# Emission order inside the turns of queries and keys: all high parts ahead of the differences that read them

## The chip, the cores and the metric

The kernel runs on one core of one Trainium2 chip. The core has five engines with queues of their own: TensorE (PE; its weight loads are listed as PEld), VectorE (DVE), ScalarE (ACT), GpSimd (POOL) and SyncE (SP, which issues DMAs). An engine carries out its instructions in the order of its queue; between engines, semaphores keep the order. The metric is the time of one execution on the device in microseconds, lower is better.

## The reference

Two trunk layers of a diffusion backbone with 512 latent tokens and 256 context tokens (768 rows of width 1024). Layer 0 mixes tokens by differential attention, layer 1 by neighbourhood attention with a position bias; each is followed by a dense MLP with squared ReLU.

```python
for i in range(DEPTH):                       # DEPTH = 2
    h_l = modulate(rms_norm(x, norm1_g[i]), mod_l[0], mod_l[1])
    h_c = modulate(rms_norm(ctx, norm1_g[i]), mod_c[0], mod_c[1])
    if kind == 0:
        y_l, y_c = diff_attention_mixer(h_l, h_c, p, i, cos, sin, need_ctx)
    elif kind == 1:
        y_l, y_c = neighbourhood_mixer(h_l, h_c, p, need_ctx)
...
    x = x + mod_l[2] * y_l
    x = x + mod_l[5] * squared_relu_mlp(modulate(rms_norm(x, norm2_g[i]), mod_l[3], mod_l[4]),
                                        w_mlp1[i], w_mlp2[i])
```

In differential attention each of 8 heads has two query and key maps of 64 channels (m = 0 and 1); the weights are the difference of two softmaxes. All arithmetic is float32.

```python
def diff_attend(q, k, v, lam):
    s = jnp.einsum('bqhmd,bkhmd->bhmqk', q, k).astype(jnp.float32) * ATTN_SCALE
    p = jax.nn.softmax(s, axis=-1)
    w = (p[:, :, 0] - lam * p[:, :, 1]).astype(v.dtype)
    return jnp.einsum('bhqk,bkhe->bqhe', w, v)
```

## The kernel before, in words

Float32 operands are multiplied as two parts: a high part, rounded by a copy on ACT to the type that PE takes (fp32r), and a low part, the difference of the value and its high part, made on DVE or POOL. Products of the parts are added in PSUM.

The time line has four phases. Layer 0's attention runs to about 470 us, layer 0's MLP to about 1110, layer 1's attention to about 1490, layer 1's MLP to the end. The attention phases are cut into steps of one head (layer 0, `head0`) or one pair of heads (layer 1, `group1`), for row tiles of 128 tokens:

- `Q`, project: PE multiplies a row tile with the head's weights (L408), ACT takes the sum out of PSUM (L415), squares (L419), DVE reduces (L421), POOL takes the power (L296), DVE scales (L423). Values are split on ACT and DVE (L468 and L469 in layer 0, L620 and L621 in layer 1). Layer 0 then rotates the channels, mostly on POOL (L473 to L483).
- `U`, turn: PE transposes queries and keys of two row tiles into one PSUM tile (L499 into PC; L634 and L636 into PA). `q_split` and `k_split` take them out in high and low parts. `U0`, `U2` and `U4` are the three turns of a head. In layer 0 tile PC has one buffer, so the next turn's transposes write over the last one's.
- `S`, scores: PE multiplies queries with keys (L517, L656), DVE takes the row maximum (L522, L662), ACT the exponential (L523, L663).
- `T`, `V`, `O`: the weights are transposed (L541, L686) and split (L543 and L544, L687 and L688), multiplied with the values (L552, L701), scaled or put together (L555 to L561, L708 and L709), and given out (L569, L570).
- `w` and `c`: loading and splitting the next head's weights (L129, then L145 on ACT and L146 on POOL, or on DVE in layer 1).

`q_split` and `k_split` work on two halves of 64 partitions, `lo` and `hi`, one for each map m. For queries, the high part of a half stays in its half and the difference goes into the other one. For keys, the high part is copied into both halves (L444, L446) and the difference too: the first on DVE (L445), the second on POOL as a copy of it (L450) in the turns U0 and U2, on DVE again in U4 (L448, `soon`). In layer 1 turn U0 has no queries, and the queries' parts are scaled by a gain (L436, L437). In each turn all these instructions but L450 read one PSUM tile.

The order of PE, SP and POOL is fixed by hand: strings such as `CYCLE0`, `START0` and `END0` list the steps ("U4' Q0b c1 w3 Q1a T0'"; a mark stands for an earlier head), and `run` emits them in this order. ACT and DVE are not fixed: a planner that simulates the program orders them when it is built, by when their inputs are ready and by the order of emission. It also sets all semaphores. Two engines' instructions that touch the same tile get an order from the order in which they are emitted.

Of the kernel before, what the change touches and what calls it, by code (L numbers as in the profile page):

```python
# [12 lines left out]
AF = mybir.ActivationFunctionType  # L13
# [50 lines left out]
class Block:  # L64
# [362 lines left out]
    def q_split(self, ps, q, cols, gain=None):  # L427

        nc = self.nc
        lo, hi = slice(0, 64), slice(64, 128)  # L430
        for m, (a, b) in enumerate(((lo, hi), (hi, lo))):
            if gain is None:
                nc.scalar.activation(q[a, m, cols], ps[a], AF.Copy)
                nc.vector.tensor_sub(q[b, m, cols], ps[a], q[a, m, cols].bitcast(F32))
            else:
                nc.scalar.activation(q[a, m, cols], ps[a], AF.Copy, scale=gain[a])  # L436
                nc.vector.scalar_tensor_tensor(q[b, m, cols], ps[a], gain[a], q[a, m, cols].bitcast(F32),  # L437
                                               op0=ALU.mult, op1=ALU.subtract)

    def k_split(self, ps, kh, kl, cols, soon):  # L440
        nc = self.nc
        lo, hi = slice(0, 64), slice(64, 128)
        for m, (a, b) in enumerate(((lo, hi), (hi, lo))):
            nc.scalar.activation(kh[a, m, cols], ps[a], AF.Copy)  # L444
            nc.vector.tensor_sub(kl[a, m, cols], ps[a], kh[a, m, cols].bitcast(F32))  # L445
            nc.scalar.activation(kh[b, m, cols], ps[a], AF.Copy)  # L446
            if soon:
                nc.vector.tensor_sub(kl[b, m, cols], ps[a], kh[a, m, cols].bitcast(F32))  # L448
            else:
                nc.gpsimd.tensor_copy(kl[b, m, cols], kl[a, m, cols].bitcast(F32))  # L450
# [679 lines left out]
```

## Time and profile before

| what | us |
|---|---|
| median of 3 runs | 1902.31 |
| lowest and highest run | 1901.79, 1906.84 |
| the profiled execution's own time | 1902.15 |
| its span, first to last instruction | 1899.6 |
| PE busy in the span | 1786.5 |
| DVE, ACT, POOL busy | 1133.4, 833.7, 812.6 |

An instruction's row in the profile names its line, the engine, the operation and the tiles it writes and reads ("Q<-PC": writes a tile Q, reads PC). A wait names the instruction that released the engine. "PE PS L517 <- ACT Q L446" means that PE stood still ahead of L517, which writes PS, until ACT's L446, which writes Q, was done. A stretch's row gives its length and then each engine's busy time in it.

### The profile page before, as it was taken

The page shows a single profiled execution, that of the slowest core. Times are in us where ns is not written, and L with a number is a line of the kernel's source. Part 1 is how long each engine was busy: PE and PEld are TensorE (multiplying, and loading weights), DVE is VectorE, ACT ScalarE, POOL GpSimd, SP SyncE. Part 2 cuts the span into 40 slices and gives each one's busy share as a digit, 9 for nine tenths or more (in the row PEclk, how much of TensorE's full clock was granted, in tenths as well). Part 3 has the DMA queues.
Part 4 walks back from the last instruction along what each step waited for, and adds up shares of the span by engine and source line. Part 5 has one row for each costly group of instructions (what it writes and reads, how often), then busy time and mean ns, then how long its engine had stood idle before and what let it go on. Part 6 is the DMA issues. An engine that isn't in the chain of part 4 may idle for free.

```text
span 1899.6 us, 27132 instructions
## 1 busy us (share of the span) xinstructions
PE 1786.5 (94%) x10256; PEld 1563.8 (82%) x10256; DVE 1133.4 (60%) x2158; ACT 833.7 (44%) x1854; POOL 812.6 (43%) x688
## 2 busy tenths in 40 slices
PE   6989999996999999999999998999998989999998
PEld 5878888884789888888888977989897778888886
DVE  4588777885574343343334676777777664444446
ACT  4476767774342212221221245777676342323321
POOL 3755566653224333342432432433345444444443
PEclk9999999997999999999999998999999999999999
DMA  8122222224324443443432132122212323223232
GB/s 329 42 84 78 87 87 87 79 71 169 119 73 136 132 160 111 167 162 116 148 134 85 56 100 64 57 71 74 65 67 89 117 92 97 89 91 109 90 101 76
DMA packets 66499, 197.61 MB, mean 104 GB/s; under 512 B 8192, under 2 KB 23488, under 8 KB 60224
## 3 DMA queue, kind: packets, MB, share of 16 engines
q1 hardware_dynamic: 58608, 186.03, 29.4%
q10 hardware_dynamic: 7760, 9.85, 1.5%
q8 instruction: 80, 1.31, 0.3%
q14 instruction: 51, 0.42, 0.1%
HBM read 180.74 MB, written 15.11 MB: 103 GB/s over the span
## 4 chain that ended last, share of the span: by engine, by line
PE 75%; DVE 11%; ACT 6%; issue 4%; POOL 2%; DMA 2%; ACTq 0%; SPq 0%; POOLq 0%; DVEq 0%
PE PD L830 22%; PE PA L408 14%; PE PA L865 11%; PE PB L865 9%; PE PA L750 4%; PE PA L257 2%; PE PS L517 2%; PE PB L552 2%; PE PQ L398 1%; PE PS L656 1%; PE PB L701 1%; PE PB L541 1%; PE PB L686 1%; DVE Y L423 1%; ACT W L145 1%
## 5 line engine op out<-in xcount | busy, mean ns | idle before, releaser
L146 POOL TENSOR_TENSOR W<-R,W 128x1024 fp32r<-128x1024 f32 x142 | 351.3, 2485 | 540.6 <-ACT W L145 537.0
L830 PE MATMUL PD<-Q,W 128*128 128x384 f32 (+2 forms) x1992 | 396.0, 346 | 2.4 <-DVE Q L334 1.1
L830 PEld LDWEIGHTS PD<-Q,W 128*128 128x128 f32 x1992 | 345.7, 188 | 33.7 <-issue 8.6
L145 ACT ACTIVATE W<-R 128x1024 fp32r<-128x1024 f32 (+1 forms) x172 | 172.7, 1021 | 450.7 <-PE PA L865 193.6
L865 PE MATMUL PA<-W,H 128*128 128x512 f32 x1080 | 275.4, 393 | 4.6 <-POOL W L146 3.0
L865 PEld LDWEIGHTS PA<-W,H 128*128 128x128 f32 x1080 | 200.1, 188 | 51.3 <-issue 4.5
L839 DVE TENSOR_TENSOR N<-N 128x768 f32<-128x768 f32 (+1 forms) x64 | 66.9, 1046 | 279.2 <-ACT N L835 170.4
L865 PE MATMUL PB<-W,H 128*128 128x512 f32 x840 | 209.2, 391 | 0.0
L865 PEld LDWEIGHTS PB<-W,H 128*128 128x128 f32 x840 | 157.4, 188 | 33.4
L408 PE MATMUL PA<-W,Q 128*128 128x384 f32 (+1 forms) x1008 | 174.3, 325 | 0.4 <-DVE H L621 0.4
L408 PEld LDWEIGHTS PA<-W,Q 128*128 128x128 f32 x1008 | 158.6, 191 | 0.7 <-DVE H L621 0.7
L296 POOL TENSOR_TENSOR SQ<-SQ,half 128x4 f32<-128x4 f32 (+1 forms) x96 | 94.7, 988 | 128.9 <-DVE SQ L421 127.7
L842 DVE SCALAR_TENSOR_TENSOR H<-N,H 128x768 fp32r<-128x768 f32 (+1 forms) x64 | 97.9, 1532 | 25.7 <-ACT H L841 25.0
L408 PE MATMUL PA<-WB,H 128*128 128x384 f32 x576 | 110.9, 345 | 0.8 <-DVE Q L469 0.8
L750 PE MATMUL PA<-W,H 128*128 128x512 f32 x384 | 97.5, 404 | 7.9 <-ACT H L743 5.1
L408 PEld LDWEIGHTS PA<-WB,H 128*128 128x128 f32 x576 | 101.1, 192 | 1.8 <-DVE Q L469 1.1
L830 PE MATMUL PD<-H,W 128*128 128x512 f32 (+1 forms) x408 | 94.1, 378 | 2.4 <-DVE SA L290 2.0
L876 DVE TENSOR_TENSOR H<-PA,H 128x512 f32<-128x512 f32 x78 | 53.8, 690 | 69.7 <-PE PA L865 69.7
L750 PEld LDWEIGHTS PA<-W,H 128*128 128x128 f32 x384 | 71.9, 192 | 25.9 <-ACT H L743 5.4
L523 ACT ACTIVATE E<-PS,SA 128x768 f32<-128x768 f32 (+1 forms) x96 | 72.9, 760 | 36.5 <-DVE SA L522 33.6
L830 PEld LDWEIGHTS PD<-H,W 128*128 128x128 f32 x408 | 73.8, 188 | 18.0 <-DVE H L334 2.9
L517 PE MATMUL PS<-Q,Q 128*128 128x256 f32 (+1 forms) x320 | 70.2, 352 | 19.1 <-ACT Q L446 9.9
(210 smaller groups left out, 3052.6 us busy)
## 6 DMA issues: line engine op xcount, KB each, us to landing
R<-in_w_dram SPq DMA_DIRECT2D x128, 512.0 KB
M<-in_wmod_dram SPq DMA_DIRECT2D x48, 1024.0 KB
R<-in_wqa_dram SPq DMA_DIRECT2D x32, 384.0 KB
R<-in_wqb_dram SPq DMA_DIRECT2D x32, 384.0 KB
Y<-in_rpb_dram SPq DMA_DIRECT2D x48, 128.0 KB
bias<-Y SPq DMA_DIRECT2D x48, 128.0 KB
X<-bias SPq DMA_DIRECT2D x8, 768.0 KB
R<-in_woa_dram SPq DMA_DIRECT2D x8, 512.0 KB
```

What stands on the lines that cost most here:

```text
L145: high = nc.scalar.activation(w[:, 0, :n], raw, AF.Copy)
L146: low = (eng or nc.gpsimd).tensor_sub(w[:, 1, :n], raw, w[:, 0, :n].bitcast(F32))
L296: nc.gpsimd.tensor_tensor(r, ss, self.half[:, :n], op=ALU.pow)
L408: nc.tensor.matmul(acc[:, :n], hT[kt][:, x, P * i:P * i + P], w[kt // 2][:, y, o:o + n], start=(kt == 0 and p == 0), stop=(kt == KT - 1 an ...
L517: nc.tensor.matmul(s[:, c0:c1], q[:, m, P * i:P * i + P], k[:, m, c0:c1], start=p == 0, stop=p == 1)
L523: nc.scalar.activation(e[:, m, :nk], s, AF.Exp, bias=mx[:, 0:1], accum_out=sm[:, m:m + 1])
L750: nc.tensor.matmul(ps, oHL[h][:, x, c:c + P], w[h // 2][:, y, 512 * (h % 2):512 * (h % 2) + 512], start=(first and h == hs[0] and p == 0), ...
L830: nc.tensor.matmul(ps[:, at:at + b1 - b0], w[kt // 4][:, x, o:o + P], hT[kt][:, y, b0:b1], start=(kt == 0 and p == 0), stop=(kt == KT - 1 ...
L839: nc.vector.tensor_mul(r, r, r)
L842: nc.vector.scalar_tensor_tensor(u[:, 1, :], r, 1.0, u[:, 0, :].bitcast(F32), op0=ALU.mult, op1=ALU.subtract)
L865: nc.tensor.matmul(ps, hd[:, x, P * i - c0:P * i - c0 + P], w[f][:, y, 512 * n:512 * n + 512], start=(f == 0 and p == 0), stop=(f == len(h ...
L876: nc.vector.tensor_add(av, ps, av)
```

## The change

In both helpers the copies of a turn are emitted ahead of the differences. In `q_split` the two copies come first, then the two differences. In `k_split` all four copies come first, then the differences (and POOL's copies) of the two halves. No instruction is added or removed, and none has other operands.

```diff
         lo, hi = slice(0, 64), slice(64, 128)
+        for m, a in enumerate((lo, hi)):
+            scale = {} if gain is None else dict(scale=gain[a])
+            nc.scalar.activation(q[a, m, cols], ps[a], AF.Copy, **scale)
         for m, (a, b) in enumerate(((lo, hi), (hi, lo))):
             if gain is None:
-                nc.scalar.activation(q[a, m, cols], ps[a], AF.Copy)
                 nc.vector.tensor_sub(q[b, m, cols], ps[a], q[a, m, cols].bitcast(F32))
             else:
-                nc.scalar.activation(q[a, m, cols], ps[a], AF.Copy, scale=gain[a])
                 nc.vector.scalar_tensor_tensor(q[b, m, cols], ps[a], gain[a], q[a, m, cols].bitcast(F32),
                                                op0=ALU.mult, op1=ALU.subtract)
...
         for m, (a, b) in enumerate(((lo, hi), (hi, lo))):
-            nc.scalar.activation(kh[a, m, cols], ps[a], AF.Copy)
+            for c in (a, b):
+                nc.scalar.activation(kh[c, m, cols], ps[a], AF.Copy)
+        for m, (a, b) in enumerate(((lo, hi), (hi, lo))):
             nc.vector.tensor_sub(kl[a, m, cols], ps[a], kh[a, m, cols].bitcast(F32))
-            nc.scalar.activation(kh[b, m, cols], ps[a], AF.Copy)
             if soon:
                 nc.vector.tensor_sub(kl[b, m, cols], ps[a], kh[a, m, cols].bitcast(F32))
             else:
```

## The prediction

> **What bounds the kernel now.** I read the page first, then the stretches, then the waits of TensorE (PE), then who holds up whom around the changed lines.
>
> ```profile
> PE 1786.5 (94%) x10256; PEld 1563.8 (82%) x10256; DVE 1133.4 (60%) x2158; ACT 833.7 (44%) x1854; POOL 812.6 (43%) x688
> ...
> 72.00:200.00 128.00, 114.24 (x713) 100.43 (x713) 101.14 (x237) 84.64 (x244) 77.89 (x94) 0.96 0.20 70
> 206.00:402.00 196.00, 189.97 (x1301) 175.63 (x1301) 156.64 (x375) 139.25 (x400) 115.77 (x150) 1.00 0.25 84
> 402.00:470.00 68.00, 51.32 (x298) 40.45 (x297) 47.53 (x98) 38.02 (x104) 29.08 (x34) 0.83 0.37 123
> ...
> 1206.00:1442.00 236.00, 218.30 (x1554) 212.95 (x1553) 182.61 (x420) 171.94 (x423) 97.14 (x113) 1.00 0.22 73
> ```
>
> PE is busy 94% of the span, and its order is written out by hand, so a faster turn of queries and keys pays only where PE stands still. The rows below the page line are stretches: length, then busy time of PE, PEld, DVE, ACT, POOL, then the granted clock. The first heads of layer 0 (72 to 200 us) leave PE idle for 13.8 us (128.00 less 114.24), its steady heads (206 to 402) for 6.0, its end (402 to 470) for 16.7, the steady groups of layer 1 (1206 to 1442) for 17.7. DVE works 77 to 80% of these stretches (end: 70%), so a wait in its queue reaches others.
>
> What ends PE's idle time, in four stretches: 72 to 205, 205 to 402, 402 to 470, then layer 1.
>
> ```profile
> PE PC L499 <- ACT Q L446: 3.3, 1, 3.3
> PE PS L517 <- ACT Q L446: 2.1, 2, 1.4
> ...
> PE PS L517 <- ACT Q L446: 3.7, 4, 1.1
> PE PS L517 <- DVE Q L448: 0.2, 1, 0.2
> ...
> PE PS L517 <- ACT Q L446: 4.1, 2, 2.5
> ...
> PE PB L686 <- DVE T L709: 6.7, 6, 1.4
> ...
> PE PS L656 <- ACT H L446: 1.1, 1, 1.1
> PE PS L656 <- DVE H L448: 0.3, 1, 0.3
> ```
>
> Columns: total, times, longest. L446 is the second high copy of the keys, the last piece of a turn. In layer 0 PE waits for it 3.3 + 2.1 + 3.7 + 4.1 = 13.2 us; in layer 1 hardly (1.1), there it waits for L709, an output step behind the turns in DVE's queue.
>
> Now ACT and DVE, layer 0 (72 to 440 us), same columns:
>
> ```profile
> ACT Q L446 <- DVE Q L445: 11.3, 10, 2.7
> ACT Q L444 <- DVE Q L434: 6.1, 7, 1.4
> ACT Q L433 <- DVE Q L434: 5.8, 10, 1.2
> ACT Q L444 <- DVE Q L448: 4.1, 6, 0.7
> ```
>
> A copy (L433, L444, L446) needs nothing that a difference makes: it reads PSUM tile PC and writes its own place. Yet it waits for the difference before it, 27.3 us in all. What they share is PC: its readers on two engines are kept one after another in the order in which they are emitted. One steady turn, step U4 of a head, shows the price:
>
> ```profile
> 234.56 0.60 PE L499 MATMUL PC<-ident,Y 128*128 128x128 f32 x4
> 235.20 0.38 ACT L433 ACTIVATE Q<-PC 64x256 fp32r<-64x256 f32 x1
> 235.61 0.42 DVE L434 TENSOR_TENSOR Q<-PC,Q 64x256 fp32r<-64x256 f32 x1
> 236.82 0.38 ACT L433 ACTIVATE Q<-PC 64x256 fp32r<-64x256 f32 x1
> 237.13 1.93 DVE L561 SCALAR_TENSOR_TENSOR O<-O,SO,one 128x128 f32<-128x128 f32 x1 [0.66 <-POOL SO L296]
> 239.09 0.43 DVE L434 TENSOR_TENSOR Q<-PC,Q 64x256 fp32r<-64x256 f32 x1
> 239.56 0.38 ACT L444 ACTIVATE Q<-PC 64x256 fp32r<-64x256 f32 x1 [0.68 <-DVE Q L434]
> 241.64 0.38 ACT L444 ACTIVATE Q<-PC 64x256 fp32r<-64x256 f32 x1 [0.74 <-DVE Q L448]
> 241.75 1.17 PE L517 MATMUL PS<-Q,Q 128*128 128x512 f32 x6
> 243.61 0.38 ACT L446 ACTIVATE Q<-PC 64x256 fp32r<-64x256 f32 x1
> 244.03 0.42 DVE L448 TENSOR_TENSOR Q<-PC,Q 64x256 fp32r<-64x256 f32 x1 [1.10 <-ACT Q L446]
> 244.05 0.96 PE L517 MATMUL PS<-Q,Q 128*128 128x512 f32 x2 [1.13 <-ACT Q L446]
> ```
>
> Six copies and six differences are 6 x 0.38 + 6 x 0.42 = 4.8 us of work; from the first copy to the end of the last difference it takes 235.20 to 244.45, 9.25 us. Each change of engine joins a queue that meanwhile does other work (the second L434 stands behind L561). PE reaches this head's scores at 241.75 and loses 1.13 us.
>
> **The change part by part.** No instruction is added, dropped or made longer; no DMA moves; the orders of PE, POOL and SP stay. What changes is the order in which the readers of a turn follow each other, and with it the plan for ACT and DVE. Call copies A, differences D.
>
> Steps U4: A D A D, then A D A D A D A D, 11 changes of engine; after, A A D D, A A A A D D D D, 3. U0 and U2 in layer 0: 8 become 3. The twelve-step chain alone stays at 4.8 us. What goes is queueing: 9.25 - 4.8 = 4.4 us over 11 changes, 0.4 each; with 3 changes the turn takes some 4.8 + 3 x 0.4 = 6.0 us, ending near 241.2, before PE's 241.75.
>
> Waits added: the first difference waits for the second copy as well, and the keys' first difference for all four copies. Without queueing the keys' first low half is ready at 4 x 0.38 + 2 x 0.42 = 2.4 us instead of 2 x 0.38 + 2 x 0.42 = 1.6: 0.8 later, the last one equal. Behind a held difference stand DVE's softmax steps and output steps. The trace shows no such block; below, a hold costs nothing where DVE has other work ahead of it, above, 0.8 us for each turn. I count 0 for the hold itself: PE's rows name copies, not first differences.
>
> Gains, by stretch:
> - Steady heads: 3.7 + 0.2 = **3.9 us**, all gone by the turn above. Late next is the exponential before the following scores, which PE waits for anyway.
> - First heads: the 2.1 goes likewise. The 3.3 is PE waiting to write the next turn over PC:
>
> ```profile
> 79.27 0.41 DVE L445 TENSOR_TENSOR Q<-PC,Q 64x256 fp32r<-64x256 f32 x1
> 81.69 0.38 ACT L446 ACTIVATE Q<-PC 64x256 fp32r<-64x256 f32 x1 [1.22 <-DVE Q L445]
> 82.13 1.11 PE L499 MATMUL PC<-ident,Y 128*128 128x128 f32 x4 [3.34 <-ACT Q L446]
> ```
>
>   With the copies done, both key differences run back to back from 79.27, ending about 80.1 instead of 82.07: 2.0. Together **4.1 us**.
> - End of layer 0: 4.1 us at stake. The copies come early, but differences still queue behind output steps; I take **2.5**, between 0 and 4.1.
> - Layer 1, steady. One group:
>
> ```profile
> 1248.36 0.39 ACT L415 ACTIVATE Y<-PA 128x256 f32<-128x256 f32 x1 [1.19 <-PE PA L408]
> 1248.94 0.38 ACT L446 ACTIVATE H<-PA 64x256 fp32r<-64x256 f32 x1
> 1249.32 0.38 ACT L444 ACTIVATE H<-PA 64x256 fp32r<-64x256 f32 x1
> 1249.73 0.85 ACT L145 ACTIVATE W<-R 128x768 fp32r<-128x768 f32 x1
> ...
> 1250.61 0.96 DVE L146 TENSOR_TENSOR W<-R,W 128x768 fp32r<-128x768 f32 x1 [0.45 <-ACT W L145]
> 1251.93 0.43 DVE L709 TENSOR_TENSOR T<-PB,T 64x256 f32<-64x256 f32 x1
> 1252.41 0.66 PE L686 MATMUL PB<-ident,E 128*128 128x128 f32 x4 [1.06 <-DVE T L709]
> ```
>
>   Two copies held back by differences stand ahead of L145, L146, L709 and so PE. Emitted together they fit into ACT's idle 1.19 us before L415, and the chain moves up by 1249.73 - 1248.94 = 0.79. I take 0.75 for each of the 6 waits: **4.5 us** (0 to 6.7).
> - End of layer 1: 1.1 + 0.3 = **1.4**.
>
> Sum 16.4. Against it: four copies in a row (1.52 us) where at most two stood (0.76), so ACT work behind can wait 0.76 longer in each of 48 turns, 36.5 us in all. The share that reaches PE I take as PE's largest idle share of a working stretch, 13.8 / 128 = 11%: **4.0 us**. Bounds: 0 (ACT's idle time takes it) and 36.5. Net 12.4. The profiled execution took 1902.15 us (span 1899.6), the median of the runs is 1902.31; 1902.15 - 12.4 = 1889.8, so **1890**.
>
> [...]
>
> **The rivals.**
> - *Only direct waits go, and the next one takes their place* (exponentials, L423 in layer 1). For it: PE has other waits close behind. Layer 0's steady 3.9 stays won, little else: 1898. Chance 0.14.
> - [...] Chance 0.03.
> - *Freed queues help more.* ACT and DVE lose most of the waits listed, and L709's 6.7 us and as much again of layer 1's idle 17.7 go: 1902.15 - 12.4 - 2.2 - 6.7 = 1881, or 1874 if half of the first heads' idle 13.8 goes too. Chance 0.13.
> - *Slower: four copies block ACT in layer 1.* Place: ahead of the exponential L663 and raw copy L415. Price 0.76 for each of 24 turns, 18.2 us; the layer's 5.9 is not won: 1902.15 - 10.5 + 18.2 = 1910. It decides when ACT has no idle time of 0.76 us ahead of these two. The idle 1.19 before L415 speaks against it, ACT's 73% share in that stretch for it. Chance 0.13.
>
> **How the numbers follow.** The forecast (1883 to 1896.5) has 0.57. The time is uncertain by some 0.3%, 5.7 us, which is what a measurement can tell from no change. Faster: 0.57 + 0.13 = 0.70; same: 0.14 + 0.03 = 0.17; slower 0.13. The range reaches from the larger gain, 1874, over the two cases at 1898 to 1906; it leaves out the slower case, 0.13, and some 0.04 below.
>
> **What would show it.** Right: no copy waits for a difference inside queries or keys; L517 waits for L446 nearly nowhere between 205 and 402 us; a U4 turn in 6 to 7 us; L499's 3.3 us cut by about 2; L686's waits for L709 under 0.5 us. Wrong: L517 waiting for L445 or L448 instead (the keys' low half is late), longer waits for L523 or L663, DVE idle for copies with its queue full behind.

## The result: slower, and the profile after

| | median us | lowest to highest | runs |
|---|---|---|---|
| before | 1903.55 | 1898.59 to 1906.84 | 7 |
| after | 1913.71 | 1909.66 to 1919.24 | 7 |

The ratio is 1.0059, 95% interval 1.0049 to 1.0070: 10 us slower, where 12 us faster were forecast, and beyond the upper end of the range, 1906. The profiled execution of the changed kernel took 1917.33 us (span 1915.5), 3.6 above its median, so its profile shows somewhat more loss than a typical run.

From here on "after" is the changed kernel. Behind the helpers its line numbers are two higher: L446 now is every copy of the keys, L433 every copy of the queries, L436 their differences in layer 0, L448 and L450 the differences of the keys, L452 POOL's copies, L519 the scores, L525 the exponential, L531 the blend of the two softmaxes, L543 its transpose, L545 and L546 the split of the weights (tile X), L571 and L572 the transpose of the output and its copy out. Later kernels shift them once more by one or a few lines; the tiles keep their names.

The page's line of busy times, after:

```profile
PE 1796.5 (94%) x10256; PEld 1568.7 (82%) x10256; DVE 1139.9 (60%) x2158; ACT 833.5 (44%) x1854; POOL 813.1 (42%) x688
```

PE itself is busy for 10 us longer than the 1786.5 of before, with the same 10256 matmuls. So in this execution the loss isn't idle time alone: matmuls have become slower (mean granted clock 0.978, before 0.981). Three stretches, cut at the same matmuls, before and then after (length, then busy time of PE, PEld, DVE, ACT, POOL, granted clock, DMA share, GB/s):

```profile
82.61:205.58 122.97, 112.43 (x707) 98.53 (x707) 96.49 (x223) 83.54 (x240) 71.17 (x87) 0.96 0.21 74
205.58:402.06 196.48, 190.45 (x1305) 176.11 (x1304) 157.12 (x375) 139.31 (x400) 116.17 (x151) 1.00 0.25 84
1110.19:1206.03 95.84, 85.41 (x498) 78.83 (x497) 67.49 (x171) 51.81 (x132) 26.97 (x33) 0.95 0.23 75
```

```profile
82.96:210.50 127.54, 112.54 (x706) 98.39 (x707) 98.90 (x230) 83.77 (x240) 73.31 (x90) 0.95 0.21 71
210.50:413.04 202.54, 191.71 (x1305) 176.36 (x1304) 165.37 (x375) 140.22 (x400) 119.17 (x150) 0.99 0.24 81
1120.77:1220.86 100.09, 86.83 (x499) 79.97 (x497) 67.50 (x172) 52.31 (x132) 26.71 (x33) 0.93 0.22 73
```

In these three, length less PE's busy time (its idle time) grows by 12.1 us and PE's busy time by 2.8: here the loss is mainly waiting. Most of the 10 us lies outside them, 3.3 of it in the first 66 us.

To compare kernels, I cut them at the same matmuls: all kernels issue the same matmuls in the same order, so a stretch of before can be found in each. This table, worked out from the traces, has the lengths for before, in us, and the change for the others, most of the experiments below among them. Its last stretch ends with the last matmul.

```
stretch of before    0-66  66-82.5  82.5-206  206-402  402-470  470-1110  1110-1206  1206-1442  1442-1490  1490-end   span
before              66.08    16.53    122.97   196.48    68.09    640.04      95.84     236.05      47.96    404.17  1899.6
after               +3.70    -3.34     +4.57    +6.06    -2.09     +1.68      +4.25      +1.73      -1.12     +0.39  1915.5
queries only        +1.48    -1.64     -0.63    -1.93    +0.43     +0.79      +0.57      -2.76      -2.06     +0.04  1893.9
keys only           -0.84    -1.67     +2.76    +2.53    -2.61     +1.70      +3.83      -1.31      -3.05     +0.14  1901.2
U4 only             +2.58    -0.20     +0.71    +0.46    -1.93     +0.79      +0.24      +1.51      +0.16     -0.35  1903.7
U0 and U2 only      +2.80    -3.34     -2.04    +3.81    +0.88     +0.78      +3.47      +0.54      -1.98     +0.41  1904.9
keys by halves      +1.60    -1.54     -2.77    -0.47    +0.38     +1.77      +0.87      -2.17      -2.19     +0.33  1895.5
four in U4          +2.44    -1.56     +2.30    +0.77    +0.81     +0.62      +0.99      -0.97      -0.01     -0.11  1905.0
four in U0, U2      +1.64    -3.34     -0.26    +3.97    -2.62     +0.78      +3.52      +0.54      -2.19     +0.36  1902.1
layer 0 only        +1.53    -3.34     +3.06    +4.03    -2.95     +4.50      +2.21      +0.41      -1.16     -0.65  1907.3
layer 1 only        +2.98    -0.20     -1.19    -0.01    +0.77     -0.13      +3.81      +1.89      -3.68     +0.80  1904.7
after, c2 late      +3.59    -3.34     +3.82    +2.07    +0.20     +1.25      +4.07      +1.69      -0.04     +0.35  1913.4
before, c2 late     +2.95    -0.21     -2.02    -0.44    -0.07     +0.84      +0.84      +0.02      -1.24     -0.66  1899.6
```

One execution each, so 2 us of a single entry mean little. The last row shows this: its kernel takes the same time as before (ratio 1.0000), yet its first stretch, which waits for the first loads, is 2.95 longer and the third 2.02 shorter. What stands out in "after" are the heads of layer 0 (+4.57 and +6.06) and the start of layer 1 (+4.25). The ends of both layers are shorter, as forecast.

The wait of the steady heads that was to go is gone, and three others stand there. PE's waits in those heads, after (210.5 to 413 us; total, times, longest):

```profile
PE PB L571 <- DVE X L546: 4.7, 4, 2.2
PE PB L543 <- DVE E L531: 3.0, 3, 1.0
PE PS L519 <- ACT E L525: 3.0, 4, 0.8
```

In the steady part of layer 1, after (1220.9 to 1458.6 us) and then, from the same view, before (1206 to 1442 us):

```profile
PE PA L636 <- DVE Y L423: 15.8, 12, 1.7
PE PB L703 <- DVE N L690: 1.7, 6, 0.3
```

```profile
PE PA L634 <- DVE Y L423: 10.6, 12, 1.5
```

The 6.7 us for the output step (L709 of before) are gone, more than the 4.5 forecast. But PE now waits 5.2 us longer for L423, the scaling of the rows that the turn's transposes read, and 1.7 us for L690.

**A last turn of a head, after.** VectorE's rows, step U4 of the head whose turn the prediction shows:

```profile
245.39 0.42 DVE L448 TENSOR_TENSOR Q<-PC,Q 64x256 fp32r<-64x256 f32 x1
245.82 0.42 DVE L450 TENSOR_TENSOR Q<-PC,Q 64x256 fp32r<-64x256 f32 x1
246.25 0.43 DVE L448 TENSOR_TENSOR Q<-PC,Q 64x256 fp32r<-64x256 f32 x1
246.69 0.43 DVE L450 TENSOR_TENSOR Q<-PC,Q 64x256 fp32r<-64x256 f32 x1
...
247.35 0.41 DVE L421 TENSOR_REDUCE SQ<-sq 128x4 f32<-128x260 f32 x1
247.69 0.74 DVE L546 TENSOR_TENSOR X<-PB,X 128x256 fp32r<-128x256 f32 x2
```

The turn's copies began at 240.80 and its last difference ends at 247.12: 6.3 us instead of 9.25, as forecast. But its four differences now run in one row of 1.73 us, and behind it stand the row statistics (L421) and the split X (L546) that PE needs for L571:

```profile
248.15 0.33 PE L571 MATMUL PB<-ident,O 128*128 128x128 f32 x1 [0.69 <-DVE X L546]
```

In before the same DVE had other work between the differences of that turn, the split of X (there L544) and the scaling L423 among it:

```profile
240.42 0.74 DVE L544 TENSOR_TENSOR X<-PB,X 128x256 fp32r<-128x256 f32 x2
241.19 0.42 DVE L448 TENSOR_TENSOR Q<-PC,Q 64x256 fp32r<-64x256 f32 x1
241.64 0.42 DVE L423 SCALAR_TENSOR_TENSOR Y<-Y,SQ 128x256 f32<-128x256 f32 x1
242.10 0.43 DVE L445 TENSOR_TENSOR Q<-PC,Q 64x256 fp32r<-64x256 f32 x1
```

**A first turn of the next head, after.** All engines, timeline, step U0:

```profile
260.78 0.96 DVE L524 TENSOR_REDUCE SA<-PS 128x1 f32<-128x768 f32 x1
260.78 1.55 ACT L446 ACTIVATE Q<-PC 64x256 fp32r<-64x256 f32 x4 [0.59 <-DVE Q L436]
...
262.36 0.37 ACT L557 ACTIVATE O<-PB,SA 128x128 f32<-128x128 f32 x1
...
262.62 0.36 ACT L572 ACTIVATE OT<-PB,subg 128x128 f32<-128x128 f32 x1
262.87 0.90 ACT L525 ACTIVATE E<-PS,SA 128x768 f32<-128x768 f32 x1
...
263.92 1.45 PE L519 MATMUL PS<-Q,Q 128*128 128x512 f32 x7 [0.74 <-ACT E L525]
```

The row maximum that the exponential needs is done at 261.74. ACT is in its row of four copies until 262.33, then two output copies follow, and the exponential starts 1.13 us after its input was ready. PE waits 0.74.

**The start of layer 1, after.** ScalarE, VectorE, then PE, step U0 of the first group:

```profile
1173.62 0.39 ACT L415 ACTIVATE Y<-PA 128x256 f32<-128x256 f32 x1 [6.33 <-PE PA L408]
...
1174.06 1.55 ACT L446 ACTIVATE H<-PA 64x256 fp32r<-64x256 f32 x4
...
1175.51 0.40 ACT L419 ACTIVATE sq<-Y 128x256 f32<-128x256 f32 x1
1175.64 0.86 DVE L448 TENSOR_TENSOR H<-PA,H 64x256 fp32r<-64x256 f32 x2 [1.14 <-ACT H L446]
...
1176.53 0.42 DVE L421 TENSOR_REDUCE SQ<-sq 128x4 f32<-128x260 f32 x1
...
1178.47 0.42 DVE L423 SCALAR_TENSOR_TENSOR Y<-Y,SQ 128x256 f32<-128x256 f32 x1
...
1178.95 0.33 PE L636 MATMUL PA<-ident,Y 128*128 128x128 f32 x1 [2.81 <-DVE Y L423]
...
1179.14 6.00 PE L408 MATMUL PA<-H,Q 128*128 128x384 f32 x24
```

And before, the same steps:

```profile
1163.20 0.39 ACT L415 ACTIVATE Y<-PA 128x256 f32<-128x256 f32 x1 [6.77 <-PE PA L408]
...
1163.90 0.41 ACT L419 ACTIVATE sq<-Y 128x256 f32<-128x256 f32 x1
...
1165.91 0.43 DVE L423 SCALAR_TENSOR_TENSOR Y<-Y,SQ 128x256 f32<-128x256 f32 x1 [0.19 <-POOL SQ L296]
...
1166.39 0.33 PE L634 MATMUL PA<-ident,Y 128*128 128x128 f32 x1 [0.67 <-DVE Y L423]
...
1166.71 4.49 PE L408 MATMUL PA<-H,Q 128*128 128x384 f32 x24
```

From the raw copy L415 to the square L419 it was 0.70 us (one key copy between), now 1.89 (four). Then two key differences stand ahead of the reduction L421 as well. L423's input is ready on POOL at 1178.04, and it starts another 0.4 us later, behind L146 and a second L421 on VectorE. L423 starts 4.85 us after L415 instead of 2.71. PE waits 2.81 us instead of 0.67, and the 24 matmuls behind that wait take 6.00 us instead of 4.49. Both together are 2.14 + 1.51 = 3.65 of the 4.25 us by which this stretch grew.

### The profile page after: what moved, and what is told of

Same layout as the page of the kernel before. It is cut to its first block, busy times and chain, and to the rows that moved or that the text cites. A ratio compares the mean times of both kernels' runs of the same rounds, so it can differ in the third digit from the quotient of the medians.

```text
span 1915.5 us, 27188 instructions
## 1 busy us (share of the span) xinstructions
PE 1796.5 (94%) x10256; PEld 1568.7 (82%) x10256; DVE 1139.9 (60%) x2158; ACT 833.5 (44%) x1854; POOL 813.1 (42%) x688
## 4 chain that ended last, share of the span: by engine, by line
PE 71%; DVE 13%; ACT 7%; issue 4%; POOL 3%; DMA 2%; ACTq 0%; SPq 0%; POOLq 0%; DVEq 0%
PE PD L832 22%; PE PA L867 11%; PE PA L408 10%; PE PB L867 9%; PE PA L752 4%; PE PA L257 2%; PE PS L519 2%; PE PB L554 2%; PE PB L703 2%; PE PQ L398 1%; PE PS L658 1%; ACT Q L446 1%; ACT E L525 1%; ACT H L446 1%; PE PB L688 1%
## 5 line engine op out<-in xcount | busy, mean ns | idle before, releaser
L146 POOL TENSOR_TENSOR W<-R,W 128x1024 fp32r<-128x1024 f32 x142 | 350.8, 2480 | 540.4 <-ACT W L145 536.9
L525 ACT ACTIVATE E<-PS,SA 128x768 f32<-128x768 f32 (+1 forms) x96 | 73.1, 761 | 35.4 <-DVE SA L524 32.4
L524 DVE TENSOR_REDUCE SA<-PS 128x1 f32<-128x768 f32 (+1 forms) x96 | 74.4, 775 | 22.3 <-PE PS L519 12.7
```

The source lines that it names most:

```text
L146: low = (eng or nc.gpsimd).tensor_sub(w[:, 1, :n], raw, w[:, 0, :n].bitcast(F32))
L524: nc.vector.tensor_reduce(mx, s, op=ALU.max, axis=AX, negate=True)
L525: nc.scalar.activation(e[:, m, :nk], s, AF.Exp, bias=mx[:, 0:1], accum_out=sm[:, m:m + 1])
```

## The experiments

Three theories stood at the start. **A:** the four key differences of a last turn (U4) in a row hold up what VectorE has behind them; through later statistics, POOL's split of weights (L146) also falls on VectorE's blend (L531) and slows it. **B:** the four key copies in a row on ScalarE hold up the exponential in the first turns (U0, U2). **C:** any other order of emission gives the planner a worse plan.

All ratios stand against runs of the kernel before on the same chip, with their 95% interval in brackets.

### The halves of the change: queries only, keys only

`e1_queries_only`: the changed kernel with the keys as before.

```diff
         for m, (a, b) in enumerate(((lo, hi), (hi, lo))):
-            for c in (a, b):
-                nc.scalar.activation(kh[c, m, cols], ps[a], AF.Copy)
-        for m, (a, b) in enumerate(((lo, hi), (hi, lo))):
+            nc.scalar.activation(kh[a, m, cols], ps[a], AF.Copy)
             nc.vector.tensor_sub(kl[a, m, cols], ps[a], kh[a, m, cols].bitcast(F32))
+            nc.scalar.activation(kh[b, m, cols], ps[a], AF.Copy)
```

> The change in the queries alone, keys as before. Theory A (the loss comes from the four key differences of a head's last turn, which now stand in a row in DVE's queue and push the value split, the X split and the statistics behind them, and with the statistics POOL's weight split into DVE's softmax blend) and theory B (the loss comes from four key copies in a row on ACT ahead of the softmax exponential, in the first turns) agree here: no row of four is left, so no loss; a few of PE's waits for L446 get shorter: 1898 to 1903. Theory C (any new emission order gives the planner a worse plan, wherever it is changed): 1907 or more.

Measured: 1895.67 us (5 runs) against 1902.53, ratio 0.9965 [0.9952, 0.9977]. Faster than before, and below the 1898 to 1903 of A and B too. Theory C falls: this is another order, and its plan isn't worse. Part of the gain goes with the granted clock, on average 0.985 in its five runs and 0.982 in the twenty of before.

`e2_keys_only`: the changed kernel with the queries as before.

```diff
-        for m, a in enumerate((lo, hi)):
-            scale = {} if gain is None else dict(scale=gain[a])
-            nc.scalar.activation(q[a, m, cols], ps[a], AF.Copy, **scale)
         for m, (a, b) in enumerate(((lo, hi), (hi, lo))):
             if gain is None:
+                nc.scalar.activation(q[a, m, cols], ps[a], AF.Copy)
...
             else:
+                nc.scalar.activation(q[a, m, cols], ps[a], AF.Copy, scale=gain[a])
```

> The change in the keys alone, queries as before. A and B: all rows of four are there, so the loss is there: 1907 to 1916. If the loss came from the queries' part: 1900 to 1904.

Measured: 1904.47 us (11 runs), ratio 1.0017 [1.0008, 1.0026]. This is less than the 1907 to 1916 that A and B expected, although all rows of four are there. The keys alone lose and the queries alone gain, but the two halves don't add up: -0.35% and +0.17% against +0.59% together. In the steady heads one difference is plain. With the keys alone PE waits 6.8 us for X and 2.4 for the blend, but not at all for the exponential; the 3.0 us for the exponential come only with both changes. How the rest of the 0.77% comes about was not settled.

### The turns: last only, first only

Both keep the helpers of before as `q_mixed` and `k_mixed` and choose by turn.

```diff
-            self.q_split(ps[:, 0:256], q, cols)
-            self.k_split(ps[:, 256:512], kh, kl, cols, i == 4)
+            q_split, k_split = (self.q_split, self.k_split) if i == 4 else (self.q_mixed, self.k_mixed)
+            q_split(ps[:, 0:256], q, cols)
+            k_split(ps[:, 256:512], kh, kl, cols, i == 4)
```

That is `e3_last_turn_only`, likewise in layer 1; `e4_first_turns_only` has `i < 4` in place of `i == 4`.

> The change in the last turn of each head alone (the one with four key differences on DVE), first two turns as before. Theory A: the loss stays, 1907 to 1914, with PE waiting for the X split and for the blend in each steady head of layer 0. Theory B: the gain of the last turn (1.1 us for each steady head) without the loss, 1893 to 1900.

> The change in the first two turns of each head alone (two key differences on DVE, two copies on POOL), last turn as before. Theory A: no loss, 1898 to 1903. Theory B: the exponentials stay late by 0.7 us in each steady head and PE still waits 1.1 us for the last turn's copies: 1907 to 1913.

Measured: last turn only 1905.84 us, ratio 1.0020 [1.0011, 1.0030] (10 runs); first turns only 1908.17, ratio 1.0032 [1.0019, 1.0044] (5 runs). Both cost, the first turns perhaps more (the intervals overlap). The last turn's time lies between the ranges of A and B, with A's mark in the steady heads: PE waits 3.5 us for X and 3.0 for the blend. The first turns' time is in B's range, but without B's mark: PE waits 1.9 us for the exponential, before 1.6, and 4.3 for the last turn's copies. So the range was met without the sign that was expected for it. In the table of stretches the growth of layer 1's start goes with the first turns (+3.47 against +0.24). Neither A nor B is the whole.

### Is it the collision of POOL's split with the blend?

In the changed kernel's steady heads, the blend beside POOL's split, and the PE row that waits for it:

```profile
254.28 1.84 POOL L146 TENSOR_TENSOR WB<-R,WB 128x768 fp32r<-128x768 f32 x1
254.90 2.04 DVE L531 SCALAR_TENSOR_TENSOR E<-E,SA 128x768 f32<-128x768 f32 x1
...
257.08 0.84 PE L543 MATMUL PB<-ident,E 128*128 128x128 f32 x6 [1.00 <-DVE E L531]
```

In the same step of before, with no instruction of POOL beside it, it took half of that:

```profile
250.16 1.01 DVE L529 SCALAR_TENSOR_TENSOR E<-E,SA 128x768 f32<-128x768 f32 x1
```

`e7_after_c2_late` moves the split (step c2) out of the way in the order that is fixed by hand.

```diff
-CYCLE0 = """w0 w1 Q0a O2'' n1' S1' O3'' V4'' V5'' c0 w2 U4' Q0b c1 w3 Q1a T0' T1' Q1b c2 O4'' S2' V0' Q2a O5'' Q2b
-S3' T2' U0 Q3a V1' c3 O0' Q3b S4' T3' Q4a Q4b V2' O1' m0 S5' T4' U2 n0 Q5a V3' Q5b m1 S0 T5'"""
+CYCLE0 = """w0 w1 Q0a O2'' n1' S1' O3'' V4'' V5'' c0 w2 U4' Q0b c1 w3 Q1a T0' T1' Q1b O4'' S2' V0' Q2a O5'' Q2b
+S3' T2' c2 U0 Q3a V1' c3 O0' Q3b S4' T3' Q4a Q4b V2' O1' m0 S5' T4' U2 n0 Q5a V3' Q5b m1 S0 T5'"""
```

> The changed kernel with one step of the steady heads' order moved: the third split of the next head's weights (c2) is emitted behind S3 and T2 instead of ahead of O4, so that POOL's weight split (L146) no longer runs beside DVE's softmax blend (L531). If the blend's 2.04 us beside the split (against 1.01 alone) are what PE waits for in each of five heads (3.0 us between the steady heads' ends in the profile): the wait L543 for L531 goes and 1909 to 1911 is left. If the statistics' delay itself costs the time, whatever POOL does: 1912 to 1916.

Measured: 1915.15 us (5 runs), ratio 1.0068 [1.0055, 1.0080] against before: no better than the changed kernel. PE's waits in its steady heads:

```profile
PE PS L519 <- ACT E L525: 3.1, 4, 0.8
...
PE PB L543 <- DVE E L531: 0.6, 3, 0.2
```

The wait for the blend did fall, 3.0 to 0.6, and the stretch was 4.0 us shorter than the changed kernel's (+2.07 instead of +6.06). But the end of layer 0 had lost its gain (+0.20 instead of -2.09), layer 1 kept its loss, and the median shows nothing of the four microseconds. The collision is real and isn't what decides; that part of theory A falls.

The same two lines changed in the kernel before (`e8_before_c2_late`) and in `e1_queries_only` (`e11_queries_c2_late`):

> The kernel before with the same move of c2. There the split and the blend do not meet (the blend takes 1.01 us), so the move alone should do nothing: 1900 to 1904.

> The change in the queries alone with c2 late. The queries alone left PE waiting 2.6 us for the blend in the steady heads, the one large wait there. If that is the meeting with POOL's weight split: it goes, 1892 to 1895. If not: as the queries alone, 1895 to 1897.

Measured: 1901.50 us, ratio 1.0000 [0.9992, 1.0009] (11 runs), and 1894.14 us, ratio 0.9964 [0.9950, 0.9977] (5 runs). The move does nothing that can be measured in either, though in the second PE's wait for the blend in the steady heads falls from 2.6 to 1.0 us. 1894.14 lies in the range expected for a gain, but its ratio is all but that of the queries alone, 0.9965; before was itself faster on this chip, 1901.68 against 1902.53.

### Rows of four, or the order as such?

`e9_keys_by_halves` keeps the queries of the change and emits the keys half by half: two copies, then that half's differences. It has no row of four.

```diff
         for m, (a, b) in enumerate(((lo, hi), (hi, lo))):
             for c in (a, b):
                 nc.scalar.activation(kh[c, m, cols], ps[a], AF.Copy)
-        for m, (a, b) in enumerate(((lo, hi), (hi, lo))):
             nc.vector.tensor_sub(kl[a, m, cols], ps[a], kh[a, m, cols].bitcast(F32))
```

> The change with the keys taken half by half: two copies, then that half's differences, then the other half's two copies. Never more than two key copies in a row on ACT nor two key differences in a row on DVE, while turns still get shorter than before. If rows of four are what costs: the loss goes, 1894 to 1901, layer 1's start within 1.5 us of before (it was 4.2 us longer). If it is the shorter turn as such that makes the planner's order worse: 1905 to 1914.

Measured: 1896.41 us (8 runs), ratio 0.9972 [0.9962, 0.9982]. One line less, and 0.59% of loss becomes 0.28% of gain. At the start of layer 1 ScalarE now has two key copies ahead of the square, and PE's wait is shorter:

```profile
1161.72 0.76 ACT L446 ACTIVATE H<-PA 64x256 fp32r<-64x256 f32 x2
...
1162.50 0.42 ACT L419 ACTIVATE sq<-Y 128x256 f32<-128x256 f32 x1
...
1165.25 0.33 PE L635 MATMUL PA<-ident,Y 128*128 128x128 f32 x1 [1.45 <-DVE Y L423]
```

The last two kernels put the rows of four back, in one kind of turn each; otherwise they are `e9_keys_by_halves`.

```diff
-        for m, (a, b) in enumerate(((lo, hi), (hi, lo))):
+        halves = list(enumerate(((lo, hi), (hi, lo))))
+        for part in ([halves] if soon else [halves[:1], halves[1:]]):
+            for m, (a, b) in part:
...
+            for m, (a, b) in part:
```

`soon` (U4) in `e12_four_in_last`, `not soon` (U0 and U2) in `e13_four_in_first`.

> Queries as in the changed kernel; keys by halves (two copies, then that half's differences) in the turns U0 and U2, all four copies ahead of the differences in U4 only. Keys by halves in every turn gave 1896.4 us, four copies ahead in every turn 1913.7, so 17.3 us are to be shared out. Theory A (rows of four on VectorE in the last turn hold up the statistics and the split of X): most of the 17 us returns here, 1906 to 1912, and TensorE's waits for X's split come back to some 4.7 us in the steady heads. Theory B (rows of four on ScalarE in the first turns hold up the exponential and, in layer 1, the square): 1896 to 1900, with the start of layer 1 (1110 to 1206 us of before) no longer than before + 1.5 us. Third theory (the two kinds of rows add up only when both are there): both this kernel and its partner below 1903.

> The partner: all four key copies ahead of the differences in U0 and U2 only, by halves in U4. Theory A: 1896 to 1900. Theory B: 1906 to 1912, with TensorE waiting some 3 us for the exponential in the steady heads and the start of layer 1 longer than before by 3 to 4 us. Third theory: below 1903, as its partner.

Measured: four in U4 1903.86 us, ratio 1.0010 [1.0000, 1.0019] (12 runs); four in U0 and U2 1905.31, ratio 1.0021 [1.0012, 1.0029] (11 runs). Against by halves, 0.9972, that is +0.38% and +0.49%; the sum +0.87% on 0.9972 gives 1.0059, the changed kernel's ratio; each difference has an interval of about 0.13% to either side. So, with the queries in the new order, the rows of four are the loss, some 7.2 us in the last turns and 9.3 us in the first (shares of 1901.19), and they add up within these intervals. The third theory of these two runs, by which the rows cost only together and both kernels stay below 1903, falls; A's row and B's row are both at work, neither as large as its own expectation. With the queries in the order of before the same rows of keys cost 0.17% (`e2_keys_only`), so this price isn't one of the rows by themselves.

Each row shows its own mark. With four in the first turns PE waits in the steady heads:

```profile
PE PB L573 <- DVE X L548: 4.1, 4, 1.7
PE PS L521 <- ACT E L527: 3.0, 4, 0.8
```

The 3.0 us for the exponential are those of the changed kernel; with four in U4, or by halves, they are not there. Nor is layer 1's start longer by more than 1 us in these two, while it grows by 3.52 with four in the first turns. With four in the last turns the wait for X is 4.6 us (by halves 3.3), and in the profiled executions the loss lies mainly in the first heads (+2.30 against -2.77). Of these 5.1 us 3.8 are PE's own busy time, at a granted clock of 0.95 against 0.99, and the execution, 1906.74 us, is the slowest of its twelve. There the row also holds up ScalarE, not VectorE alone:

```profile
137.08 1.55 ACT L448 ACTIVATE Q<-PC 64x256 fp32r<-64x256 f32 x4 [0.43 <-DVE Q L436]
...
137.63 0.30 PE L573 MATMUL PB<-ident,O 128*128 128x128 f32 x1 [0.25 <-DVE O L565]
...
139.82 0.37 ACT L574 ACTIVATE OT<-PB,subg 128x128 f32<-128x128 f32 x1
...
140.24 0.55 PE L545 MATMUL PB<-ident,E 128*128 128x128 f32 x3 [1.98 <-ACT OT L574]
```

PE's transpose of the output is done at 137.93. Its copy L574 comes 1.9 us later, behind the four copies and what was queued after them, and PE waits 1.98 for tile PB. (By halves the same wait is 1.20.) What part of U4's 7.2 us is ScalarE's row and what part VectorE's can't be told from these runs, since in this turn one row follows the other.

### The layers

`e5_layer0_only` and `e6_layer1_only` use the changed helpers in one layer and `q_mixed` and `k_mixed` in the other. Layer 0's choice and layer 1's, for the first of them:

```diff
+            q_split, k_split = (self.q_split, self.k_split) if True else (self.q_mixed, self.k_mixed)
...
+                (self.q_split if False else self.q_mixed)(
...
+            (self.k_split if False else self.k_mixed)(
```

In the second True and False change places.

> The changed order in layer 0 alone, the order of before in layer 1. The changed kernel's stretches between 66 and 545 us of before were 6.8 us longer than before's, those of layer 1 (1110 to 1541) 4.5 us, the start 3.7 (which differs from run to run). If the stretches tell it, layer 0 alone gives before + 5 to + 9, 1907 to 1911. The rival of the prediction (four copies block ScalarE in layer 1, price 18 us there) would have layer 0 alone faster than before, some 1890 to 1897.

> The changed order in layer 1 alone. By the stretches before + 3 to + 6: 1905 to 1908, with nearly all of it in the layer's start. By the prediction's rival 1913 to 1921. If the layers add up, this one's loss and the other's make 10 us together.

Measured: layer 0 only 1907.16 us, ratio 1.0034 [1.0022, 1.0046] (5 runs); layer 1 only 1905.96, ratio 1.0026 [1.0016, 1.0036] (8 runs). The layers add up to 0.60%. The loss isn't layer 1's alone, as the prediction's slower rival had it. Which layer costs more isn't settled: the intervals overlap, and in the profiled execution of layer 0 only 4.50 us of the growth lie in the MLP stretch, 470 to 1110, whose instructions the change leaves as they were.

Against before, by halves (0.9972), queries only (0.9965) and the latter with the late c2 (0.9964) are faster. Their intervals overlap, so none of the three is shown to be the best.

## Why the prediction was wrong

**The waits it named did go.** L517's wait for L446 in the steady heads: 3.7 to nothing. L499's 3.3, which the prediction cut by 2.0: its stretch (66 to 82.5 us) is 3.34 shorter. The end of layer 0: 2.09 shorter, forecast 2.5. L686's 6.7: gone, forecast 4.5. The end of layer 1: 1.12, forecast 1.4. A U4 turn takes 6.3 us, forecast 6 to 7.

**One item of its list was missed in part.** Key copies still wait for query differences ("ACT Q L446 <- DVE Q L436", 10.6 us from 72 to 440), since keys and queries share the PSUM tile. The prediction's list counted only copies behind the differences of their own kind as the sign. Two of its signs of being wrong did come: PE's wait for the exponential in the steady heads went from 1.6 to 3.0 us, and VectorE's wait for the key copies in layer 1 (1150 to 1470 us) from 8.5 to 22.1.

**The steps that failed are the two that priced the rows.** The first is "I count 0 for the hold itself", because PE's rows name copies and not first differences. The second is the term for four copies in a row, 0.76 us for each of 48 turns at PE's largest idle share, 11%: 4.0 us. If the 16.4 us of gains are taken as won in full, the 10.2 us of loss leave 26.6 for these two terms. That is an estimate, but the runs measure the like: putting the rows of four back into the kernel by halves costs 7.2 + 9.3 = 16.5 us. Both numbers lie within the 0 to 36.5 us that the prediction gave as the bounds of the second term, and far from the value it took. The runs don't part the two terms, since a row of copies also holds the first difference behind it.

Why was 11% wrong? It was called PE's largest idle share of a working stretch, but the end of layer 0, in the same list, is idle for 16.7 of 68 us, 25%, and was left out without a reason; even that would have given only 9.0 us. More to the point, PE's idle share says how much of the time PE already waits. It doesn't say how often an instruction that PE is about to wait for stands right behind a turn in ACT's or DVE's queue. By the runs 16.5 of the 36.5 us came through, 45%, with VectorE's rows and the clock in that number. The plan of before had put the exponential, the square, the statistics and the split of X between the pieces of a turn; the waits of the copies for the differences were the gaps in which that work ran. In the rows of before quoted above, the split of X and L423 stand between the differences. So the 4.4 us of "queueing" in a U4 turn, which the prediction read as loss, were in good part other work, and some of it, the split of X above all, PE needed just as soon. The prediction's own sentence, that the work behind a held difference is DVE's softmax and output steps, was right; its price of zero was not.

**A second effect wasn't in the sum:** the granted clock. Behind the wait of 2.81 us at the start of layer 1 the same 24 matmuls took 6.00 us instead of 4.49; 1.51 of the 3.65 us there are of this kind, and PE's busy time grew by 10 us in the profiled execution. That execution has the lowest clock of its seven, 0.978; their mean is 0.981, against 0.982 in the runs of before on the other chips. One less the clock, times the span, is 35.5 us on average for the changed kernel and 33.5 to 34.5 for before: by this estimate the clock is 1 to 2 of the 10 us in a typical run, and waiting the rest.

**The rivals.** "Four copies block ACT" came nearest, 1910 against 1913.7. Its mechanism was there, but it put the place in layer 1 alone, ahead of L663 and L415, at 18.2 us. Measured, layer 1 alone costs 4.8 us (1905.96 less 1901.19), its mark is the square L419 and then L423, and layer 0 costs as well (6.0 us); VectorE's row is a second part. The reason held against it, that the idle 1.19 us ahead of L415 would take the copies, was read at one place in one group. "Only direct waits go, the next takes their place" is what the steady part of layer 1 shows: 6.7 us gone, 5.2 us more for L423 and 1.7 for L690. "Freed queues help more" was right that all 6.7 us go, and had nothing of the waits that came. The chance of 0.03 stands for a case at 1898 us that no run shows: in before the second query copy waits for the first difference, in the other half of the partitions (L433 for L434, 5.8 us in 10 waits), and the new order of the queries alone gained 0.35%.

## What to carry to other kernels

In this kernel a wait between two engines that have queues full of other work wasn't lost time as long as that work ran in the gap (in the last turn of before shown above the split of X, 0.74 us, and L423, 0.42 us). Before counting a chain's shortening as a gain, list what ran in its gaps, and ask for each item whether the bounding engine waits for it next. Where several results become ready together, emit them in groups no larger than the slack of the instruction behind them: here two copies and their differences at a time gained 0.28%, four at a time lost 0.59%, with the same instructions.

## What the runs showed of the hardware

**A wait of 2.81 us cost another 1.5 us of clock.** In the changed kernel and in the five others whose copies in the first turns of layer 1 stand four in a row, PE waits 2.81 us at that place, and the next 24 matmuls take 6.00 or 6.01 us. With the waits of 0.67 to 1.46 us that before, queries only, keys by halves, four in U4 and layer 0 only have there the same 24 took 4.47 to 4.49. In the traces of before and after the granted clock is 1.00 or 0.50 and, but for the piece that the end of the trace cuts short, changes in steps of 3.41 us. Two of them, after, the wait in the first (length, PE's busy time, granted clock, DMA share, GB/s):

```profile
1176.51:1179.92 3.41, 0.97 (x6) 1.00 0.19 33
1179.92:1183.34 3.42, 3.42 (x12) 0.50 0.21 82
```

PE was busy for 0.97 of the 3.41 us ahead of the drop.

The fourteen traces together show how busy PE was ahead of a drop. From 60 us on, all 123 steps at full clock in which PE was busy for less than 45% are followed by one at half clock, and none of the 7028 in which it was busy for 57% or more (in before and after alone: all 18, and none of 1007); in between both occur. So a wait need not last a whole step: by an estimate from these shares and the 3.41 us, one of 1.5 to 1.9 us can be enough if it falls into a single step, while the same wait spread over two steps costs nothing more.

**VectorE's blend took 2.04 us beside POOL's split and 1.01 alone.** In the rows above the blend started 0.62 us into the split and ended 0.82 after it. Moving the split away took PE's wait for the blend from 3.0 to 0.6 us and made the kernel no faster.
